# Two half-step FFNs by seven block products: the token sums made feature-major instead of token-major

## The chip, the cores and the metric

The kernel runs on one core of a Trainium2 chip. The metric is the device time of one launch in microseconds, taken as the median of several runs. PE is the matrix engine, DVE the vector engine, ACT the scalar engine, POOL the GpSimd engine, SP the engine whose queue issues most transfers.

## The reference, cut to what matters

One layer of a decoder is computed for 1024 prompt tokens, 16 learned meta tokens and 64 sample tokens (1104 rows of 1024 features, the second half-step 1088 rows):

```
def rms_norm(x, g):
    y = x * rsqrt(mean(x * x, -1) + 1e-6)
    return y * g

def swiglu(x, w_gate, w_up, w_down):          # 1024 -> 2816 -> 1024
    return (silu(x @ w_gate) * (x @ w_up)) @ w_down

def half_ffn(h, g_pre, g_post, w_gate, w_up, w_down):
    return h + 0.5 * rms_norm(swiglu(rms_norm(h, g_pre), w_gate, w_up, w_down), g_post)

h = half_ffn(h, ffn1 ...)                     # first half-step
h = h + rms_norm(token_mixer(...), g)         # DeltaNet and windowed attention, merged by w_out
h = half_ffn(h, ffn2 ...)                     # second half-step
```

## The kernel before

**Seven products.** Each half-step (class `Ffn`) multiplies by blocks in the manner of Strassen and Winograd. The features are cut into halves 1 and 2 (512 each), the tokens into a first half (token tiles 0 to 3 and one half of tile 8) and a second half (tiles 4 to 7 and the other half of tile 8). Tile t of the first half (x) and tile t + 4 of the second half (y) stand at the same columns. Seven operands are made of x1, x2, y1, y2: product 1 takes x1, product 2 x2, product 4 y2, product 5 y1 + y2 - x1 ... by the code, with s = y1 + y2: 5 takes s, 7 takes x1 - y1, 6 takes s - x1, 3 takes x2 - (s - x1). Every operand is feature-major (features on partitions, tokens along the row) and split into a high part and a low part (`x40h`, `x40l`: product 4, columns part 0, high and low), so that three matmuls give an accurate product.

**Making the operands.** The normalised rows of a tile are token-major. `place` (before, L202 to L211) turns 512 features of a tile by four PE transposes into one PSUM buffer (`tr`, four of them in a ring; I call the four transposes a set), ACT copies them to the high part (L210), DVE subtracts to get the low part (L211). `left` does this for x1 and x2 of a first-half tile: two sets. `right` first makes the sums token-major (L230: two on DVE, two on POOL, the POOL ones in place in x) and then turns five things, y2, s, x1 - y1, s - x1 and x2 - (s - x1): five sets, with a yield behind each.

**The order of the work.** PE's order is written by hand: `weave` mixes generators, each with a begin, an end and a count of steps. A half-step begins with `start(0)`, products 1 and 2 of the first column block of gate and up, in two column parts (part 0 needs tiles 0 and 1, part 1 tiles 2, 3 and 8), and `start(1)`, the same of the next column block with both parts in each step. The sets of the tiles are woven in between. In the first half-step that is `tiles_in`: ten steps of `left` before and in part 0 of `start(0)`, then ten steps of `right` (tiles 4 and 5) in part 1, ten (tiles 6 and 7) in `start(1)`, and tile 8's five behind it. Then `up` goes on with products 6, 5, 7, 4, 3, which need all tiles. In the second half-step `right` of tiles 4 and 5 and `left` of 0, 1, 2 and 8 run in `Merge.run`, beside the output projection (matmuls into `dn`) of a later tile, and tiles 6, 3, 8 and 7 in `Merge.rest`, beside `start`. The token tiles of the merge come in the order 0, 4, 1, 5, 2, 8, 6, 3, 7. Tiles 2 and 8 are written to DRAM (`kept`) in `finish` and read again in `rest`, because their place in SBUF is used by others.

**The other engines.** DVE, ACT, POOL and SP each run their queue strictly in the order in which the build's scheduler put it. For each weight block ACT makes the high part (`wh`, L281) and POOL the low part (`wl`, L282). A tile is normalised by a square with row sum on ACT (L81), two small POOL operations (L82, and a power, L83) and a scaling on DVE (L90). In the merge a tile passes through ACT copies out of PSUM, a square, POOL's power, DVE (L623), POOL's addition of the residual (L624), a store to DRAM (L1794), and then L81 to L90 again. DVE also makes the low part of the projection's input (L1750).

Of the kernel before, what the change touches and what calls it, by code (L numbers as in the profile page):

```python
# [13 lines left out]
ALU = mybir.AluOpType  # L14
# [20 lines left out]
def f32(ap):  # L35
    return ap.bitcast(F32)
# [50 lines left out]
def normed(c, pool, x, n, g, dump=None, pin=lambda op: op):  # L87

    r = rstd(c, pool, x, n, 1.0 / D, EPS, "n", dump, pin)
    pin(c.nc.vector.scalar_tensor_tensor(out=x[:n], in0=x[:n], scalar=r[:n, 0:1], in1=g[:n], op0=ALU.mult,  # L90
                                         op1=ALU.mult))
# [79 lines left out]
class Ffn:  # L171
# [28 lines left out]
            lo, hi = self.parts[i]  # L200
            self.X[p][i] = tuple(self.c.t(pool, [P, 4, hi - lo], F32R, tag=f"x{p}{i}{x}") for x in "hl")

    def place(self, psum, p, i, o, src, n):

        c, nc = self.c, self.nc
        ps = c.t(psum, [P, 4, P], tag="tr")
        for k in range(4):
            nc.tensor.transpose(ps[:, k, :n], src[:n, k * P:(k + 1) * P], c.ident[:n, :n])  # L208
        hi, lo = (x[:, :, o:o + n] for x in self.X[p][i])
        nc.scalar.copy(hi, ps[:, :, :n])  # L210
        nc.vector.tensor_tensor(out=lo, in0=ps[:, :, :n], in1=f32(hi), op=ALU.subtract)  # L211

    def where(self, t):

        return (1, 256, self.tail) if t == 8 else (t % 4 // 2, t % 2 * P, P)

    def left(self, psum, x, t):

        i, o, n = self.where(t)
        for p, h in ((1, 0), (2, 512)):  # L220
            self.place(psum, p, i, o, x[:, h:h + 512], n)
            yield

    def right(self, pool, psum, x, y, t):

        nc = self.nc
        i, o, n = self.where(t)
        x1, x2, y1, y2 = x[:n, 0:512], x[:n, 512:], y[:n, 0:512], y[:n, 512:]
        s = self.c.t(pool, [P, 512], tag="sum", bufs=2)[:n]
        op = lambda e, out, a, b, o: e.tensor_tensor(out=out, in0=a, in1=b, op=o)  # L230
        op(nc.vector, s, y1, y2, ALU.add)
        op(nc.vector, y1, x1, y1, ALU.subtract)
        op(nc.gpsimd, x1, s, x1, ALU.subtract)
        op(nc.gpsimd, x2, x2, x1, ALU.subtract)
        for p, src in ((4, y2), (5, s), (7, y1), (6, x1), (3, x2)):
            self.place(psum, p, i, o, src, n)
            yield


    def raw(self, kind, fs, names, pin=lambda op: op):  # L240
# [378 lines left out]
def post_add(c, pool, y, n, g, res, dump):  # L619

    nc = c.nc
    r = rstd(c, pool, y, n, 1.0 / D, 4.0 * EPS, "p", dump)
    nc.vector.scalar_tensor_tensor(out=y[:n], in0=y[:n], scalar=r[:n, 0:1], in1=g[:n], op0=ALU.mult, op1=ALU.mult)  # L623
    nc.gpsimd.tensor_tensor(out=y[:n], in0=y[:n], in1=res[:n], op=ALU.add)  # L624
# [74 lines left out]
class Mixer:  # L699
# [1005 lines left out]


class Merge:
# [80 lines left out]
    def finish(self, t, n, o, dump):  # L1788
        c, nc, pool = self.c, self.nc, self.pool
        t0 = TILES[t][0]  # L1790
        res = c.t(pool, [P, D], tag="res")
        nc.sync.dma_start(res[:n], self.h1_d[t0:t0 + n])
        post_add(c, pool, o, n, self.gain("mix_norm_post", pool), res, dump)
        nc.sync.dma_start(self.h2_d[t0:t0 + n], o[:n])  # L1794
        normed(c, pool, o, n, self.gain("ffn2_norm_pre", pool), res)
        self.o[t] = o
        if t in (2, 8):
            self.kept[t] = c.t(self.f2_d, [P, D], tag="kept", bufs=2)
            nc.sync.dma_start(self.kept[t][:n], o[:n])

    def feed(self, t):

        if t in (4, 5):
            return self.f2.right(self.pool, self.f2.ptr, self.o[t - 4], self.o[t], t), 5
        return self.f2.left(self.f2.ptr, self.o[t], t), 2

    def rest(self):

        pool, right = self.pool, self.f2.right
        x2, x8, y8 = (f32(self.c.t(pool, [P, H, P], F32R, tag=tag)).rearrange("p h t -> p (h t)")  # L1810
                      for tag in ("yl", "yl", "yh"))
        n = self.f2.tail
        for x, src in ((x2, self.kept[2]), (x8[:n], self.kept[8][:n]), (y8[:n], self.kept[8][n:2 * n])):
            self.nc.sync.dma_start(x, src)
        yield from right(pool, self.f2.ptr, x2, self.o[6], 6)
        yield from self.feed(3)[0]
        yield from right(pool, self.f2.ptr, x8, y8, 8)
        yield from right(pool, self.f2.ptr, self.o[3], self.o[7], 7)

# [37 lines left out]
    def run(self, f2, es):  # L1857
        c = self.c
        self.f2, self.o, self.kept = f2, {}, {}
        self.pool = c.pool(es, "mo", bufs=2)  # L1860
        self.f2_d = c.pool(es, "keptd", space=DRAM)
        pso = ExitStack()
        self.psum = c.pool(pso, "pso", space=PSUM, side="right")
        order = (0, 4, 1, 5, 2, 8, 6, 3, 7)
        y = self.load(order[1])
        self.finish(0, P, self.o0, c.t(self.pool, [P, H, P], F32R, tag="yh").rearrange("p h t -> p (h t)"))
        for i in range(1, 9):
            if i == 5:
                f2.ahead(self.pool, "yl")
            now, y = y, self.load(order[i + 1]) if i < 8 else None  # L1870
            done = []
            if i > 1 and order[i - 2] != 6:
                g, n = self.feed(order[i - 2])
                done = [(g, 0.6, 0.95, n)]
            o = c.t(*((self.first, [P, H, P], F32R, "yh") if i % 3 == 0 else (self.pool, [P, H, P], F32R, "o")))
            weave((self.tile_(order[i], *now, f32(o).rearrange("p h t -> p (h t)")), 0, 1, 33 if order[i] == 8 else 49), *done)
        pso.close()


def body(tc, I, O):  # L1880
    nc = tc.nc
    with ExitStack() as es:
        es.enter_context(tc.manual_schedule(engines={mybir.EngineType.PE}))
        c = Ctx(tc)
# [12 lines left out]
        def gain(name, pool):  # L1897
            if name not in gains:
# [289 lines left out]
```

## Time and profile before

| what | value |
|---|---|
| median of 3 runs | 2671.67 us (2671.36, 2671.67, 2674.96) |
| the profiled execution's own time | 2667.11 us |
| its span | 2665.3 us |
| granted PE clock, mean | 0.994 |
| busy: PE, DVE, POOL, ACT | 98%, 58%, 49%, 42% |
| first half-step's start, `start` and the sets of all tiles | 9 to 62 us |
| merge with sets of tiles 0, 4, 1, 5, 2, 8 | 1845 to 1932 us |
| second half-step's `start` with tiles 6, 3, 8, 7 | 1932 to 1970 us |

The profiled execution lies 1.8 us above its span and 4.6 us under the median. A row of a timeline gives the start in us, the busy time in us (of a single instruction, from its start to its end; the next one on the engine can start before), the engine, line, operation and tiles, and in brackets the idle time before it with what ended it. A row of the table by stage gives the stage, the length, and busy time with the count of instructions for PE, PE's weight loads, DVE, ACT, POOL, then the granted clock, the DMA share and GB/s.

### The profile page before, as it was taken

The page shows a single profiled execution, that of the slowest core. Times are in us where ns is not written, and L with a number is a line of the kernel's source. Part 1 is how long each engine was busy: PE and PEld are TensorE (multiplying, and loading weights), DVE is VectorE, ACT ScalarE, POOL GpSimd, SP SyncE. Part 2 cuts the span into 40 slices and gives each one's busy share as a digit, 9 for nine tenths or more (in the row PEclk, how much of TensorE's full clock was granted, in tenths as well). Part 3 has the DMA queues.
Part 4 walks back from the last instruction along what each step waited for, and adds up shares of the span by engine and source line. Part 5 has one row for each costly group of instructions (what it writes and reads, how often), then busy time and mean ns, then how long its engine had stood idle before and what let it go on. Part 6 is the DMA issues. An engine that isn't in the chain of part 4 may idle for free. (4 is left out here: it accounts for less than half of the span.)

```text
span 2665.3 us, 49487 instructions
## 1 busy us (share of the span) xinstructions
PE 2601.2 (98%) x19053; PEld 2478.5 (93%) x19053; DVE 1547.3 (58%) x2299; ACT 1125.8 (42%) x2718; POOL 1293.5 (49%) x1221
## 2 busy tenths in 40 slices
PE   7999999999999999999999999999999999999998
PEld 7999999999988999888889999997799999999998
DVE  7656565545676726995454444444556656654566
ACT  6333343432145634457444444454443434334221
POOL 6656555445526733433343333435555555554471
PEclk9999999999999999999999999999999999999999
DMA  4344343667544754345333333335433434338764
GB/s 164 121 152 153 126 167 117 243 228 252 189 151 149 220 161 132 110 121 171 98 103 89 91 94 100 100 93 160 150 121 139 166 127 149 128 139 317 243 226 144
DMA packets 229568, 406.46 MB, mean 153 GB/s; under 512 B 59750, under 2 KB 121350, under 8 KB 229046
## 3 DMA queue, kind: packets, MB, share of 16 engines
q1 hardware_dynamic: 209030, 324.75, 37.8%
q10 hardware_dynamic: 20304, 78.56, 7.4%
q8 instruction: 150, 2.46, 0.4%
q14 instruction: 84, 0.69, 0.1%
HBM read 264.36 MB, written 140.53 MB: 152 GB/s over the span
## 5 line engine op out<-in xcount | busy, mean ns | idle before, releaser
L132 PE MATMUL gu<-xh,wl 128*128 128x512 f32 (+3 forms) x1456 | 493.6, 339 | 0.0
L128 PE MATMUL gu<-xh,wh 128*128 128x512 f32 (+3 forms) x1456 | 490.5, 337 | 0.0
L130 PE MATMUL gu<-xl,wh 128*128 128x512 f32 (+3 forms) x1456 | 490.3, 337 | 0.0
L282 POOL TENSOR_TENSOR wl<-T,wh 128x512 fp32r<-128x512 f32 x246 | 331.2, 1353 | 320.2 <-ACT wh L281 248.4
L496 PE MATMUL y<-hb,wh 128*128 128x256 f32 (+2 forms) x2528 | 430.5, 290 | 2.4 <-ACT acc L536 1.0
L282 POOL TENSOR_TENSOR wl<-raw,wh 128x512 fp32r<-128x512 f32 x200 | 282.8, 1422 | 249.5 <-ACT wh L281 183.2
L496 PEld LDWEIGHTS y<-hb,wh 128*128 128x128 f32 x2528 | 365.9, 188 | 3.6 <-DVE acc L507 1.4
L281 ACT CAST wh<-T 128x512 fp32r<-128x512 f32 x246 | 152.1, 620 | 364.5 <-PE B L316 111.3
L130 PEld LDWEIGHTS gu<-xl,wh 128*128 128x128 f32 x1456 | 275.9, 190 | 16.7 <-issue 0.6
L128 PEld LDWEIGHTS gu<-xh,wh 128*128 128x128 f32 x1456 | 276.0, 190 | 16.5 <-issue 0.9
L132 PEld LDWEIGHTS gu<-xh,wl 128*128 128x128 f32 x1456 | 276.0, 190 | 16.4 <-issue 0.4
L496 PE MATMUL y<-hb,wl 128*128 128x256 f32 (+2 forms) x1264 | 271.6, 288 | 0.0
L281 ACT CAST wh<-raw 128x512 fp32r<-128x512 f32 x200 | 122.4, 620 | 276.4 <-PE C L316 82.6
L507 DVE TENSOR_TENSOR acc<-acc,y 128x552 f32<-128x552 f32 (+4 forms) x216 | 144.9, 679 | 139.3 <-PE y L496 138.9
L770 POOL TENSOR_TENSOR wl<-raw,wh 128x1024 fp32r<-128x1024 f32 x58 | 139.7, 2409 | 162.0 <-ACT wh L769 132.4
L496 PEld LDWEIGHTS y<-hb,wl 128*128 128x128 f32 x1264 | 207.0, 188 | 0.0
L256 DVE TENSOR_TENSOR T<-raw,raw 128x512 f32<-128x512 f32 x124 | 117.5, 952 | 108.6 <-POOL wl L282 108.6
L1564 POOL TENSOR_TENSOR f<-f,mhalf 128x1 f32<-128x1 f32 (+1 forms) x72 | 54.6, 758 | 125.6 <-DVE f L1562 123.7
L267 DVE TENSOR_TENSOR T<-raw,T 128x512 f32<-128x512 f32 x62 | 65.5, 1060 | 60.8 <-POOL wl L282 60.7
L930 DVE SCALAR_TENSOR_TENSOR cv<-pc,cw,cv 128x1131 f32<-128x1131 f32 x48 | 66.8, 1394 | 31.1 <-POOL cv L927 30.7
L256 DVE TENSOR_TENSOR T<-raw,T 128x512 f32<-128x512 f32 x62 | 63.2, 1027 | 31.9 <-POOL wl L282 31.5
L769 ACT CAST wh<-raw 128x1024 fp32r<-128x1024 f32 x60 | 62.9, 1048 | 32.8 <-PE gu L130 32.8
(593 smaller groups left out, 7325.1 us busy)
## 6 DMA issues: line engine op xcount, KB each, us to landing
hb<-hid SPq DMA_DIRECT2D x71, 552.0 KB
hb<-hid SPq DMA_DIRECT2D x71, 544.0 KB
hid<-hs ACTq DMA_DIRECT2D x69, 552.0 KB
hid<-hs ACTq DMA_DIRECT2D x69, 544.0 KB
raw<-in_w_in_dram SPq DMA_DIRECT2D x58, 512.0 KB
raw<-in_ffn_w_gate_dram SPq DMA_DIRECT2D x100, 256.0 KB
raw<-in_ffn_w_up_dram SPq DMA_DIRECT2D x94, 256.0 KB
raw<-in_ffn_w_down_dram SPq DMA_DIRECT2D x88, 256.0 KB
```

Source lines behind the costliest of these rows:

```text
L128: nc.tensor.matmul(ps, wh, xh, start=first and i == 0, stop=False)
L130: nc.tensor.matmul(ps, wh, xl, start=False, stop=False)
L132: nc.tensor.matmul(ps, wl, xh, start=False, stop=last and i == n - 1)
L256: pin(self.nc.vector.tensor_tensor(out=b[name], in0=b[x], in1=b[y], op=ALU.subtract))
L267: nc.vector.tensor_tensor(out=s, in0=b["21"], in1=s, op=ALU.subtract)
L281: self.nc.scalar.copy(hi, s)
L282: self.nc.gpsimd.tensor_tensor(out=lo, in0=s, in1=f32(hi), op=ALU.subtract)
L496: self.nc.tensor.matmul(self.view(ps[d], (i,)), w[x][:, d * P:(d + 1) * P], hb[:, y, lo:hi], start=j + x + y == 0, stop=j == len(items) - ...
L507: dve = lambda out, x, y: nc.vector.tensor_tensor(out=out, in0=x, in1=y, op=ALU.add)
L769: nc.scalar.copy(hi, raw)
L770: low.tensor_tensor(out=lo, in0=raw, in1=f32(hi), op=ALU.subtract)
L930: nc.vector.scalar_tensor_tensor(out=cv, in0=pc[:, w:w + PADW], scalar=self.cw[:, j, w:w + 1], in1=cv, op0=ALU.mult, op1=ALU.add)
```

## The change

`place` is cut in two: `turned` makes a set, and `place` takes any feature-major source, in PSUM or in SBUF. `left` turns x1 and x2 as before and in addition copies each set, by ACT, over the tile's own token-major values, so that x is kept feature-major in its own place. `right` turns only y2 and y1. The sums are then made feature-major: s3 = x1 - y1 and s2 = y2 - s3 on DVE (one input of each in PSUM, the results in two `sum` buffers, of which there are two in all), x1 + s2 and x2 - s2 on POOL in place in x. Products 7, 6, 5 and 3 are placed from these, from SBUF. A `right` has two steps in place of five, so the weaves of both half-steps take other counts and places. `kept` now holds the feature-major x of tiles 2 and 8 (for tile 8 in pieces of 32 tokens), written behind `left`; tile 8's y rows go to DRAM by themselves.

```
-    def place(self, psum, p, i, o, src, n):
-        ps = c.t(psum, [P, 4, P], tag="tr")
+    def turned(self, psum, src, n):
+        ps = self.c.t(psum, [P, 4, P], tag="tr")
         for k in range(4):
+            self.nc.tensor.transpose(ps[:, k, :n], src[:n, k * P:(k + 1) * P], self.c.ident[:n, :n])
+        return ps[:, :, :n]
+
+    def place(self, p, i, o, src):
+        hi, lo = (x[:, :, o:o + src.shape[2]] for x in self.X[p][i])
+        self.nc.scalar.copy(hi, src)
+        self.nc.vector.tensor_tensor(out=lo, in0=src, in1=f32(hi), op=ALU.subtract)
...
     def left(self, psum, x, t):
-        for p, h in ((1, 0), (2, 512)):
-            self.place(psum, p, i, o, x[:, h:h + 512], n)
+        for p, h, own in zip((1, 2), (0, 512), self.halves(x, n)):
+            ps = self.turned(psum, x[:, h:h + 512], n)
+            self.place(p, i, o, ps)
+            self.nc.scalar.copy(own, ps)
             yield
     def right(self, pool, psum, x, y, t):
-        op(nc.vector, s, y1, y2, ALU.add)
-        op(nc.vector, y1, x1, y1, ALU.subtract)
-        op(nc.gpsimd, x1, s, x1, ALU.subtract)
-        op(nc.gpsimd, x2, x2, x1, ALU.subtract)
-        for p, src in ((4, y2), (5, s), (7, y1), (6, x1), (3, x2)):
-            self.place(psum, p, i, o, src, n)
-            yield
+        y2 = self.turned(psum, y[:, 512:], n)
+        self.place(4, i, o, y2)
+        yield
+        y1 = self.turned(psum, y[:, 0:512], n)
+        op(nc.vector, s3, x1, y1, ALU.subtract)
+        op(nc.vector, s2, y2, s3, ALU.subtract)
+        op(nc.gpsimd, x1, x1, s2, ALU.add)
+        op(nc.gpsimd, x2, x2, s2, ALU.subtract)
+        self.place(7, i, o, s3)
+        self.place(6, i, o, s2)
+        self.place(5, i, o, x1)
+        self.place(3, i, o, x2)
+        yield
...
     def left(self, t):
+        yield from self.f2.left(self.f2.ptr, self.o[t], t)
         if t in (2, 8):
+            x, n = self.o[t], self.f2.where(t)[2]
+            self.kept[t] = self.c.t(self.f2_d, [P, KD, P], tag="kept", bufs=2)
+            self.nc.sync.dma_start(self.kept[t][:, :, :n], x.rearrange("p (k t) -> p k t", t=P)[:, :, :n])
...
-        weave((first, 0, 1, 49), (steps_of(tr, 10), 0.1, 0.9, 10))
-        weave((f1.start(1, False), 0, 1, 49), (steps_of(tr, 10), 0.1, 0.9, 10))
+        weave((first, 0, 1, 49), (steps_of(tr, 4), 0.1, 0.9, 4))
+        weave((f1.start(1, False), 0, 1, 49), (steps_of(tr, 4), 0.05, 0.85, 4))
...
-        weave((steps_of(first, 48), 0, 1, 48), (steps_of(rest, 7), 0.25, 0.95, 7))
-        weave((first, 0, 1, 49), (steps_of(rest, 5), 0.1, 0.8, 5))
-        weave((f2.start(1, False), 0, 1, 49), (steps_of(rest, 5), 0.1, 0.8, 5))
+        weave((steps_of(first, 48), 0, 1, 48), (steps_of(rest, 4), 0.25, 0.9, 4))
+        weave((first, 0, 1, 49), (steps_of(rest, 2), 0.2, 0.7, 2))
+        weave((f2.start(1, False), 0, 1, 49), (steps_of(rest, 2), 0.1, 0.6, 2))
```

The scheduler orders the other engines anew in these stages and nowhere else, but for one transfer of the mixer that changes places with its neighbour. Three places of the new order matter to the prediction.

DVE in the first half-step, where tiles 4 and 5 are placed; `x_416` (before) and `x_415` (after) are the rows of tile 6, whose normalisation is the L90 row. Before:

```order
L211 TENSOR_TENSOR x30l_76<-tr_405,x30h_75 128x4x128
L211 TENSOR_TENSOR x40l_83<-tr_429,x40h_82 128x4x128
L90 SCALAR_TENSOR_TENSOR x_416<-x_416,rn_418,g_ffn_norm_pre_143 128x1024
L211 TENSOR_TENSOR x50l_104<-tr_440,x50h_103 128x4x128
L211 TENSOR_TENSOR x70l_97<-tr_451,x70h_96 128x4x128
```

There the scaling of tile 6 stood directly behind the first low part of tile 5, `x40l`. DVE at the same place after:

```order
L239 TENSOR_TENSOR sum_424<-tr_425,sum_423 128x512
L214 TENSOR_TENSOR x50l_104<-x_36_139,x50h_103 128x4x128
L214 TENSOR_TENSOR x70l_97<-sum_423,x70h_96 128x4x128
L214 TENSOR_TENSOR x30l_76<-x_36_139,x30h_75 128x4x128
L214 TENSOR_TENSOR x60l_111<-sum_424,x60h_110 128x4x128
L214 TENSOR_TENSOR x50l_104<-x_37_141,x50h_103 128x4x128
L90 SCALAR_TENSOR_TENSOR x_415<-x_415,rn_417,g_ffn_norm_pre_143 128x1024
```

It now stands behind `x50l` of tile 5 (the one with `x_37`), which needs POOL's sum of that tile.

POOL at the same place after; `x_36` and `x_37` are tiles 0 and 1, in which the sums of tiles 4 and 5 are made, `rn_417` is tile 6's factor, and "x2" is x1 + s2 with x2 - s2:

```order
L297 TENSOR_TENSOR wl_575<-raw_472,wh_574 128x512
L239 TENSOR_TENSOR x_36_139<-x_36_139,sum_369 128x512 x2
L297 TENSOR_TENSOR wl_623<-raw_476,wh_622 128x512
L82 TENSOR_SCALAR rn_417<-rn_417 128x1
L239 TENSOR_TENSOR x_37_141<-x_37_141,sum_424 128x512 x2
L83 TENSOR_TENSOR rn_417<-rn_417,mhalf_64 128x1
```

Tile 6's power now stands behind both sums of tile 5; before, its two operations followed each other directly.

DVE in the merge after, around the projection input of tile 6 (`yl_22160`, L1765, L1750 before) and the scaling of tile 2 (`o_22057`, L638, L623 before):

```order
L214 TENSOR_TENSOR x20l_21725<-tr_22111,x20h_21724 128x4x128
L638 SCALAR_TENSOR_TENSOR o_22057<-o_22057,rp_22128,g_mix_norm_post_21778 128x1024
L1765 TENSOR_TENSOR yl_22160<-yl_22160,yh_22161 128x1024
L214 TENSOR_TENSOR x40l_21720<-tr_22194,x40h_21719 128x4x128
L239 TENSOR_TENSOR sum_22192<-o_21871,tr_22206 128x512
```

Before, the row of L1750 stood two rows ahead of that of L623; now it stands behind it.

More of the change, by code (lines that the diff above doesn't have):

```diff
@@ L201, in x_tiles, with halves @@
             self.X[p][i] = tuple(self.c.t(pool, [P, 4, hi - lo], F32R, tag=f"x{p}{i}{x}") for x in "hl")
-    def place(self, psum, p, i, o, src, n):
-        c, nc = self.c, self.nc
-        ps = c.t(psum, [P, 4, P], tag="tr")
+    def turned(self, psum, src, n):
+        ps = self.c.t(psum, [P, 4, P], tag="tr")
         for k in range(4):
[L208 to L211, printed above, removed]
+            self.nc.tensor.transpose(ps[:, k, :n], src[:n, k * P:(k + 1) * P], self.c.ident[:n, :n])
[4 more added lines that the diff above has]
+        self.nc.vector.tensor_tensor(out=lo, in0=src, in1=f32(hi), op=ALU.subtract)
     def where(self, t):
         return (1, 256, self.tail) if t == 8 else (t % 4 // 2, t % 2 * P, P)
+    def halves(self, x, n):
+        return [x[:, h:h + 512].rearrange("p (k t) -> p k t", t=P)[:, :, :n] for h in (0, 512)]
     def left(self, psum, x, t):
         i, o, n = self.where(t)
-        for p, h in ((1, 0), (2, 512)):
-            self.place(psum, p, i, o, x[:, h:h + 512], n)
+        for p, h, own in zip((1, 2), (0, 512), self.halves(x, n)):
+            ps = self.turned(psum, x[:, h:h + 512], n)
+            self.place(p, i, o, ps)
+            self.nc.scalar.copy(own, ps)
             yield
@@ L227, in right @@
         i, o, n = self.where(t)
-        x1, x2, y1, y2 = x[:n, 0:512], x[:n, 512:], y[:n, 0:512], y[:n, 512:]
-        s = self.c.t(pool, [P, 512], tag="sum", bufs=2)[:n]
+        x1, x2 = self.halves(x, n)
+        s3, s2 = (self.c.t(pool, [P, 4, P], tag="sum", bufs=2)[:, :, :n] for _ in range(2))
         op = lambda e, out, a, b, o: e.tensor_tensor(out=out, in0=a, in1=b, op=o)
-        op(nc.vector, s, y1, y2, ALU.add)
-        op(nc.vector, y1, x1, y1, ALU.subtract)
-        op(nc.gpsimd, x1, s, x1, ALU.subtract)
-        op(nc.gpsimd, x2, x2, x1, ALU.subtract)
-        for p, src in ((4, y2), (5, s), (7, y1), (6, x1), (3, x2)):
-            self.place(psum, p, i, o, src, n)
-            yield
+        y2 = self.turned(psum, y[:, 512:], n)
[11 more added lines that the diff above has]
+        yield
     def raw(self, kind, fs, names, pin=lambda op: op):
@@ L1796, in finish, with left @@
         self.o[t] = o
-        if t in (2, 8):
-            self.kept[t] = c.t(self.f2_d, [P, D], tag="kept", bufs=2)
-            nc.sync.dma_start(self.kept[t][:n], o[:n])
+        if t == 8:
+            self.kept_y = c.t(self.f2_d, [P, D], tag="kept_y")
+            nc.sync.dma_start(self.kept_y[:n // 2], o[n // 2:n])
     def feed(self, t):
         if t in (4, 5):
-            return self.f2.right(self.pool, self.f2.ptr, self.o[t - 4], self.o[t], t), 5
-        return self.f2.left(self.f2.ptr, self.o[t], t), 2
+            return self.f2.right(self.pool, self.f2.ptr, self.o[t - 4], self.o[t], t)
+        return self.left(t)
+    def left(self, t):
+        yield from self.f2.left(self.f2.ptr, self.o[t], t)
+        if t in (2, 8):
+            x, n = self.o[t], self.f2.where(t)[2]
+            self.kept[t] = self.c.t(self.f2_d, [P, KD, P], tag="kept", bufs=2)
+            self.nc.sync.dma_start(self.kept[t][:, :, :n], x.rearrange("p (k t) -> p k t", t=P)[:, :, :n])
     def rest(self):
@@ L1812, in rest @@
         n = self.f2.tail
-        for x, src in ((x2, self.kept[2]), (x8[:n], self.kept[8][:n]), (y8[:n], self.kept[8][n:2 * n])):
-            self.nc.sync.dma_start(x, src)
+        for x, t, n in ((x2, 2, P), (x8, 8, n)):
+            self.nc.sync.dma_start(x.rearrange("p (k t) -> p k t", t=P)[:, :, :n], self.kept[t][:, :, :n])
+        self.nc.sync.dma_start(y8[:n], self.kept_y[:n])
         yield from right(pool, self.f2.ptr, x2, self.o[6], 6)
-        yield from self.feed(3)[0]
+        yield from self.feed(3)
         yield from right(pool, self.f2.ptr, x8, y8, 8)
@@ L1872, in run @@
             if i > 1 and order[i - 2] != 6:
-                g, n = self.feed(order[i - 2])
-                done = [(g, 0.6, 0.95, n)]
+                done = [(self.feed(order[i - 2]), 0.6, 0.95, 2)]
             o = c.t(*((self.first, [P, H, P], F32R, "yh") if i % 3 == 0 else (self.pool, [P, H, P], F32R, "o")))
```

## Prediction

> **What bounds the kernel now.** I read the page first, then PE's timeline in the stages that the change touches, then the table by stage.
>
> ```profile
> span 2665.3 us, 49487 instructions
> PE 2601.2 (98%) x19053; PEld 2478.5 (93%) x19053; DVE 1547.3 (58%) x2299; ACT 1125.8 (42%) x2718; POOL 1293.5 (49%) x1221
> ```
>
> ```profile
> 1967.14 3.02 PE C L316 x24
> ```
>
> PE is busy 98% of the span; the last line, from the chain that ended last, is the steady state (24 matmuls in 3.02 us, 0.126 each). So an edit pays through PE's own instructions or through PE's waits. PE's waits in the touched stages, and where the first half-step's products 6 begin:
>
> ```profile
> 27.80 0.41 PE L316 MATMUL A<-x11l,wh 128*128 128x296 f32 x1 [1.58 <-DVE x11l L211]
> 61.54 0.39 PE L316 MATMUL B<-x60h,wh 128*128 128x256 f32 x1
> 1894.38 0.63 PE L208 MATMUL tr<-ident,o 128*128 128x128 f32 x4 [0.77 <-DVE x40l L211]
> 1908.94 0.50 PE L132 MATMUL dn<-xh,yl 128*128 128x512 f32 x1 [0.43 <-DVE yl L1750]
> 1940.14 1.09 PE L208 MATMUL tr<-ident,yl 128*128 128x128 f32 x4 [2.07 <-DVE x41l L211]
> 1945.91 0.40 PE L316 MATMUL A<-x11h,wh 128*128 128x288 f32 x1 [1.03 <-ACT x11h L210]
> 1946.63 0.40 PE L316 MATMUL A<-x11l,wh 128*128 128x288 f32 x1 [0.33 <-DVE x11l L211]
> ```
>
> A wait has a second price. The table by stage gives per stretch its length, busy time and count of PE, PEld, DVE, ACT, POOL, then the granted clock, DMA share and GB/s:
>
> ```profile
> 25.30:28.70 3.40, 1.30 (x7) 1.09 (x8) 3.40 (x8) 0.66 (x3) 0.00 (x0) 0.99 0.00 0
> 28.70:32.10 3.40, 3.40 (x17) 3.37 (x16) 2.73 (x3) 1.61 (x3) 3.30 (x3) 0.50 0.00 0
> 57.50:61.50 4.00, 1.91 (x21) 1.54 (x20) 3.18 (x8) 1.13 (x4) 2.53 (x2) 1.00 0.68 249
> 62.80:66.20 3.40, 3.40 (x17) 3.40 (x16) 3.37 (x5) 1.22 (x2) 1.61 (x2) 0.50 0.63 204
> 1936.70:1940.10 3.40, 1.37 (x12) 1.16 (x11) 2.59 (x4) 0.95 (x2) 1.77 (x1) 1.00 0.00 0
> 1940.10:1943.50 3.40, 3.36 (x16) 3.39 (x17) 2.38 (x4) 2.21 (x3) 3.32 (x3) 0.50 0.03 5
> ```
>
> Each stretch in which PE is busy less than half is followed by 3.4 us at a granted clock of 0.50, which loses half of it, 1.7 us.
>
> **The change, part by part.** All times are on the profiled execution's scale, 2667.11; the median is 4.6 higher.
>
> *Sets.* The price of a set of four transposes, from a place where PE has no wait:
>
> ```profile
> 32.15 0.29 PE L316 MATMUL C<-x11h,wl 128*128 128x296 f32 x1
> 32.28 0.60 PE L208 MATMUL tr<-ident,x 128*128 128x128 f32 x4
> 32.64 0.38 PE L316 MATMUL C<-x11h,wh 128*128 128x296 f32 x1
> 32.86 0.29 PE L316 MATMUL C<-x11l,wh 128*128 128x296 f32 x1
> 32.99 0.30 PE L316 MATMUL C<-x11h,wl 128*128 128x296 f32 x1
> ```
>
> From 32.15 to 32.99 PE started three matmuls and a set; matmuls alone start every 0.133 (32.86 to 32.99), so the set costs 0.84 - 3 x 0.133 = 0.44 us. Five right tiles in each of two half-steps lose three sets each: 30 sets, 13.2 us, if PE is the bound wherever they stood. The Trainium skill, "TensorE: Matmul & The Clock Gate", Part 4 (PE-mode transpose), gives about 275 ns for one transpose in a kernel's context; by it the 120 transposes would be an estimated 33 us. The row has four of them in 0.60 busy, so they overlap, and I keep 0.44.
>
> *New work on a shared port.* Before, the low parts (L211) took one input from PSUM. After, those of products 7, 6, 5 and 3 take both from SBUF. What two SBUF inputs on DVE cost beside POOL:
>
> ```profile
> 28.72 1.60 POOL L230 TENSOR_TENSOR x<-sum,x 128x512 f32<-128x512 f32 x1 [3.85 <-DVE x L230]
> 30.40 1.61 POOL L230 TENSOR_TENSOR x<-x 128x512 f32<-128x512 f32 x1
> 29.21 1.65 DVE L230 TENSOR_TENSOR x<-x,x 128x512 f32<-128x512 f32 x1
> 30.79 0.68 DVE L211 TENSOR_TENSOR x40l<-tr,x40h 128x512 fp32r<-128x512 f32 x1
> ```
>
> DVE's sum at 29.21, both inputs in SBUF, ends 0.54 behind the end of POOL's (30.32) and takes 1.65; the low part from PSUM at 30.79 runs beside POOL's next sum in its usual 0.68. So such a DVE instruction and a POOL one exclude each other. The Trainium skill, "SBUF — State Buffer", Who interferes with whom, states this as an exclusive lock for the whole instruction; the rows agree. A right tile had two such DVE instructions and has four now, and their times and POOL's must be added.
>
> *First half-step: +10.5.*
>
> ```profile
> 12.37 0.60 ACT L210 CAST x10h<-tr 128x512 fp32r<-128x512 f32 x1
> 12.84 0.61 ACT L210 CAST x20h<-tr 128x512 fp32r<-128x512 f32 x1
> 13.32 1.09 ACT L81 ACTIVATE dump<-x 128x1024 bf16<-128x1024 f32 x1
> 33.23 1.28 POOL L282 TENSOR_TENSOR wl<-raw,wh 128x512 fp32r<-128x512 f32 x1
> 34.47 1.29 POOL L230 TENSOR_TENSOR x<-x 128x512 f32<-128x512 f32 x1
> 38.18 0.55 POOL L83 TENSOR_TENSOR rn<-rn,mhalf 128x1 f32<-128x1 f32 x1
> 38.94 1.27 DVE L90 SCALAR_TENSOR_TENSOR x<-x,rn,g_ffn_norm_pre 128x1024 f32<-128x1024 f32 x1
> 40.13 0.68 DVE L211 TENSOR_TENSOR x50l<-tr,x50h 128x512 fp32r<-128x512 f32 x1
> ```
>
> (a) Four of `left`'s own copies stand on ACT ahead of tile 2's square. Copies follow each other by 0.48 (12.37, 12.84, 13.32): 1.9 us, so the part 1 that began at 27.80 begins near 29.7. (b) From there PE has 47 matmuls at 0.133, four sets at 0.44, one cold stretch (1.7) and 14 matmuls at 0.127 before tile 6's first set: it asks for tile 6 at 29.7 + 6.3 + 1.8 + 1.7 + 1.8 = 41.3. (c) Tile 6's scaling now stands on DVE behind the `x50l` of tile 5, which needs POOL's sum x1 + s2 of tile 5; that needs s2, which needs one of the two `sum` buffers, free only when tile 4's low parts and POOL's second sum of tile 4 are done. Its power stands on POOL behind both sums of tile 5. ACT's high part of the second weight block stands behind the copy of A (24 matmuls, two sets and the cold stretch behind 29.7), so POOL is done with the low part (1.28) near 36.9, an estimate. From there on the port: POOL four sums at 1.25, one more weight low part at 1.25 and the small operations at 0.75, together 7.0; DVE six low parts at 0.6 and the scaling at 1.25 with waits for the high parts, together 5.4. 36.9 + 12.4 = 49.3, and PE stands for 8.0 us in place of nothing. Without any exclusion only the longer chain counts, and PE would stand 4.2. (d) From 49.3 the remaining port work of tiles 6, 7 and 8 is 6 sums at 1.25, a weight low part at 1.25, and on DVE 10 low parts and two weight sums at 0.6 and one scaling at 1.25, together 17.4 (12 x 0.6 + 1.25 + 7 x 1.25 = 17.2 and a small operation). About 4 us more pass while one waits for the other's result or for PE's set, and the last high and low part of product 6, which DVE has behind everything else, take 1.3. Products 6 begin near 72.0 and not at 61.54: +10.5. PE's 15 removed sets (6.6) vanish in this wait. Bounds: without exclusion, and with tile 6 4.2 late, less the sets, +2.8; with twice the idle, +13. I take 10.5, since the row at 29.21 shows the exclusion.
>
> *Merge: +2 (0 to +3.5).* Six sets (2.6) and the wait of 0.77 at 1894.38 go.
>
> ```profile
> 1907.68 1.21 DVE L1750 TENSOR_TENSOR yl<-yl,yh 128x1024 fp32r<-128x1024 f32 x1
> ```
>
> But PE already waits at 1908.94 for this low part, which ends at 1908.89. PE arriving earlier only waits longer there. The chain to it (tile 2's norm, its residual, the store and load, the squares of tile 8) gets `kept` copies and own copies put ahead, about 1.6 us on ACT and DVE; and tile 2's scaling now stands ahead of tile 6's projection input, 1.27 more of which I count a third. So the wait grows by what the sets gave back and the stage ends 2 later. A wait of 2 could also cost a cold stretch. The Trainium skill, "TensorE: Matmul & The Clock Gate", What's actually happening, has the clock go cold after an idle window of about 3.4 us; by it this wait would be free of that. The row at 1936.70 went cold after a wait of 2.07 with other idle time near it, so I keep 3.5 as the upper end.
>
> *Second half-step's start: -8.6.* In 1932 to 1970 nine sets go (4.0), the wait of 2.07 at 1940.14 goes because `tr` buffers turn over less, and with it the cold stretch (1.7); the waits of 1.03 and 0.33 for tile 3 go if its low part is in time: -9.1. What is late next is that low part:
>
> ```profile
> 1929.44 1.74 POOL L230 TENSOR_TENSOR yl<-sum,yl 128x512 f32<-128x512 f32 x1
> 1934.79 0.55 POOL L83 TENSOR_TENSOR rp<-rp,mhalf 128x1 f32<-128x1 f32 x1
> 1938.12 1.27 DVE L623 SCALAR_TENSOR_TENSOR o<-o,rp,g_mix_norm_post 128x1024 f32<-128x1024 f32 x1
> 1941.84 2.36 POOL L624 TENSOR_TENSOR o<-o,res 128x1024 f32<-128x1024 f32 x1
> ```
>
> Behind tile 7's power (ends 1935.34) DVE does its scaling (1.27), then tile 6's `x41l` and two sums (0.6 each, an input in PSUM), to 1938.5; `x71l` excludes POOL's residual of tile 7 (2.36 from 1936.7) and ends at 1939.7, and tile 3's `x11l` follows at 1940.3. PE, without the waits, asks for it at 1945.91 less 2.07, 1.7, three sets (1.3) and 1.03, at 1939.8. That gives +0.5 back.
>
> Sum: 10.5 + 2 - 8.6 = +3.9, so 2671.0 for the profiled execution and **2675.6** on the median's scale. 0.2%, 5.3 us, is about what a measurement of this kernel can tell from no change.
>
> **The rivals.** *Faster, by PE's own sum.* If the walk in the first half-step is wrong and PE is never late there: 15 sets less the 1.9 of the copies, -4.7; merge -2.6 - 0.77 = -3.4; start -8.6; together -16.7, 2655. For it speaks that DVE, POOL and ACT are 58%, 49% and 42% busy; against it that PE is already 1.58 late at 27.80 with less on those engines. A weaker form, in which the exclusion costs nothing: 2.8 + 0 - 8.6 = -5.8, 2665.9.
>
> *Slower, by the second half-step.* The same exclusion holds tile 3's `x11l`: if POOL's first sum of tile 6 (1.74) too gets the port ahead of `x71l`, `x11l` ends 1.74 + 2.36 = 4.1 later, and the wait brings a cold stretch back (1.7): +5.8 on top of the forecast, 2681.4. It decides as soon as `x11l` of tile 3 ends more than 7.7 us behind the merge's last matmul (near 1932.1); my walk has 8.2. With the first half-step at its ceiling it is 2684.
>
> *The turned sums do nothing to the ends*: gains and losses cancel as in the forecast, but within 5.3 of 2671.67.
>
> **How the numbers follow.** The forecast's sum stands inside the bound of "same" (2666.3 to 2677.0), with its own range 2668 to 2680, from the first half-step's and the merge's bounds. Faster: 0.13 for PE's plain sum, 0.15 for the weaker form, 0.28. The forecast within the bound: 0.38. Slower: 0.34, of which 0.2 is the second half-step's rival and the rest the upper bounds of the first half-step and the merge. The range leaves out the plain sum's 0.13 and some 0.06 above: 2661 to 2685.
>
> **What would show it.** Right: in the changed profile a PE wait of some 8 us near 41 to 50 for tile 6's first set, released by DVE's scaling L90; products 6 near 72; DVE low parts of L214 with two SBUF inputs of 1.2 to 1.9 us beside POOL's sums; 1932 to 1970 shorter by 8 to 9 with no clock of 0.50 in it. Wrong: products 6 at or ahead of 61 (no hold-up), low parts at 0.68 throughout (no exclusion), a `start` in the second half-step that still waits for `x11l`, or a merge that ends earlier by 2 or more.

## The result, and the profile after

The changed kernel takes 2688.70 us (median of 5 runs, 2683.83 to 2693.48) beside 2671.67 for the kernel before: a ratio of 1.0053, with a 95% interval of 1.0042 to 1.0064, slower by some 14 us by the ratio (its interval is 11 to 17) and 17 by the medians. The prediction said 2675.6 and at most 2685. The profiled execution after is 2688.70 itself, its span 2686.9, and it is 21.6 longer than that of before.

The same parts of the page, after:

```profile
span 2686.9 us, 49248 instructions
PE 2594.4 (97%) x18933; PEld 2471.5 (92%) x18933; DVE 1555.3 (58%) x2299; ACT 1135.7 (42%) x2738; POOL 1290.7 (48%) x1221
```

PE has 120 instructions less and is busy 6.8 us less: the sets are gone. Its idle time (the span less the busy time) has grown from 64.1 to 92.5, by 28.4. PE's timeline after, the rows with a wait in the two stages, and the row at which the second one ends:

```profile
30.13 0.61 PE L331 MATMUL A<-x11h,wh 128*128 128x296 f32 x1 [1.87 <-ACT x11h L213]
50.41 1.08 PE L207 MATMUL tr<-ident,x 128*128 128x128 f32 x4 [7.06 <-DVE x L90]
68.65 0.55 PE L331 MATMUL B<-x60h,wh 128*128 128x256 f32 x1 [3.49 <-DVE sum L239]
72.06 0.61 PE L331 MATMUL B<-x61h,wh 128*128 128x296 f32 x1 [2.86 <-ACT x61h L213]
1892.10 0.80 PE L128 MATMUL dn<-xh,yh 128*128 128x512 f32 x1 [5.76 <-ACT yh L1873]
1923.67 0.79 PE L128 MATMUL dn<-xh,yh 128*128 128x512 f32 x1 [8.86 <-ACT o L1870]
1969.80 0.40 PE L331 MATMUL A<-x11h,wh 128*128 128x288 f32 x1 [1.17 <-ACT g L363]
1990.77 0.28 PE L331 MATMUL B<-x60h,wh 128*128 128x256 f32 x1
```

The first four rows are the hold-up of the first half-step that was forecast. Products 6 begin there in two column parts, with `x60h` at 68.65 (61.54 before) and, behind a further wait, with `x61h` at 72.06 (61.76 before). The wait for tile 6 that ends at 50.41 is DVE's and POOL's; DVE, then POOL after:

```profile
39.80 1.77 DVE L214 TENSOR_TENSOR x60l<-sum,x60h 128x512 fp32r<-128x512 f32 x1
48.99 1.27 DVE L90 SCALAR_TENSOR_TENSOR x<-x,rn,g_ffn_norm_pre 128x1024 f32<-128x1024 f32 x1
```

```profile
44.66 3.26 POOL L239 TENSOR_TENSOR x<-x,sum 128x512 f32<-128x512 f32 x2
47.88 1.00 POOL L83 TENSOR_TENSOR rn<-rn,mhalf 128x1 f32<-128x1 f32 x1
```

The power (L83) stands behind both sums of tile 5, and the scaling (L90) begins 0.1 behind its end.

The two waits of some 6 and 9 us in the merge were not: there PE waits to begin the next tile's projection, and is released by ACT's copy of the last tile out of `dn` (two buffers, each for half the features of a tile). In the second half-step's start the waits of 2.07, 1.03 and 0.33 of before have become one of 1.17. The table by stage, first the kernel before, then after; the stages are the merge (first to last projection matmul) and the start (from there to the first matmul of product 6):

```profile
1833.30:1931.90 98.60, 96.74 (x440) 76.49 (x441) 51.00 (x50) 44.75 (x77) 48.24 (x49) 0.98 0.48 156
1931.90:1970.00 38.10, 34.67 (x263) 33.02 (x262) 18.25 (x29) 19.50 (x39) 18.41 (x16) 0.96 0.36 122
```

```profile
1848.80:1960.80 112.00, 97.38 (x416) 76.95 (x417) 51.08 (x47) 48.54 (x85) 44.31 (x48) 0.91 0.43 138
1960.80:1990.80 30.00, 28.78 (x227) 27.80 (x226) 23.85 (x30) 19.30 (x39) 18.95 (x16) 1.00 0.48 151
1886.40:1889.80 3.40, 0.00 (x0) 0.00 (x0) 3.23 (x4) 1.37 (x3) 3.04 (x2) 1.00 0.34 77
1889.80:1893.20 3.40, 1.10 (x3) 0.91 (x4) 1.49 (x2) 2.32 (x4) 0.25 (x1) 0.50 0.00 0
1893.20:1896.60 3.40, 3.40 (x10) 2.63 (x9) 1.89 (x2) 1.14 (x3) 0.97 (x3) 0.50 0.20 28
```

The merge has grown by 13.4, the start has shrunk by 8.1. In the merge PE's clock is 0.91 in the mean: the last two rows show it at 0.50 from 1889.80 to 1896.60. The first 2.3 of these 6.8 us still lie in the first wait; for the other 4.5 the matmuls have begun again and are slow. Around the second wait the clock is at 0.50 from about 1917.1 to 1927.3, of which 3.6 lie behind the wait. The Trainium skill, "TensorE: Matmul & The Clock Gate", What's actually happening, has the clock go cold behind one idle window of about 3.4 us; the trace agrees for this wait (the stretch from 1886.40 has no PE work at all).

With the first matmul of product 5 as the first half-step's mark (66.22 before, 77.65 after), the difference of 21.6 is made of +11.4 in the first half-step, +4.1 up to the merge, +13.4, -8.1, and +0.8 behind it. The 4.1 lie in the mixer, where nothing was changed but two transfers that changed places; the ten experiments below are longer there by 0.7 to 7.1 than the profiled execution before, which lies under all five timed runs of its kernel. So the three stages carry 16.7, about the 17.0 between the medians; that the 4.1 belong to this execution of the kernel before, and not to the change, is argued from this and not shown.

Why PE waits in the merge is read from the engines that come before the copy. PE's last set of tile 4 and of tile 5, then ACT, DVE and POOL after, from tile 4's last set to the copy, with the second copy as ACT's last row (the `yh` of L239, L214 is tile 0's place, where x1 + s2 and x2 - s2 of tile 4 are made; the `yh` that L1873 writes is tile 5, in the same place):

```profile
1884.35 0.60 PE L207 MATMUL tr<-ident,o 128*128 128x128 f32 x4
1913.28 0.60 PE L207 MATMUL tr<-ident,yh 128*128 128x128 f32 x4
```

```profile
1882.69 0.59 ACT L213 CAST x40h<-tr 128x512 fp32r<-128x512 f32 x1 [0.35 <-PE tr L207]
1888.41 0.62 ACT L213 CAST x50h<-yh 128x512 fp32r<-128x512 f32 x1 [1.15 <-POOL yh L239]
1890.08 0.62 ACT L213 CAST x30h<-yh 128x512 fp32r<-128x512 f32 x1 [1.05 <-POOL yh L239]
1891.46 1.07 ACT L1873 COPY yh<-dn 128x512 f32<-128x512 f32 x2 [0.76 <-DVE x30l L214]
1923.03 1.07 ACT L1870 COPY o<-dn 128x512 f32<-128x512 f32 x2 [1.67 <-DVE x30l L214]
```

```profile
1884.00 1.28 DVE L90 SCALAR_TENSOR_TENSOR o<-o,rn,g_ffn_norm_pre 128x1024 f32<-128x1024 f32 x1
1885.92 0.69 DVE L239 TENSOR_TENSOR sum<-tr,sum 128x512 f32<-128x512 f32 x1
1887.30 1.63 DVE L214 TENSOR_TENSOR x60l<-sum,x60h 128x512 fp32r<-128x512 f32 x1
1890.73 0.69 DVE L214 TENSOR_TENSOR x30l<-yh,x30h 128x512 fp32r<-128x512 f32 x1
```

```profile
1886.76 3.30 POOL L239 TENSOR_TENSOR yh<-yh,sum 128x512 f32<-128x512 f32 x2 [3.51 <-DVE sum L239]
```

The copy ends a chain: set, sums on DVE, two sums on POOL, high part, low part of product 3, and only then is the place free. It takes 7.1 us for tile 4 (1884.35 to 1891.46) and 9.75 for tile 5 (1913.28 to 1923.03). The kernel before at the same copy, ACT:

```profile
1871.91 0.59 ACT L1850 COPY yh<-dn 128x512 f32<-128x512 f32 x1 [0.78 <-PE tr L208]
1872.87 0.61 ACT L1850 COPY yh<-dn 128x512 f32<-128x512 f32 x1
```

There the sums were made ahead of the sets, and the last one to read the place was PE's own transposition, so the copy came directly behind it and PE never waited for it; for the copy into tile 1's place it waited 0.26.

### The profile page after: what moved, and what is told of

It is laid out like the page before. It is cut to its first block, busy times and chain, and to the rows that moved or that the text cites. A ratio compares the mean times of both kernels' runs of the same rounds, so it can differ in the third digit from the quotient of the medians.

```text
span 2686.9 us, 49248 instructions
## 1 busy us (share of the span) xinstructions
PE 2594.4 (97%) x18933; PEld 2471.5 (92%) x18933; DVE 1555.3 (58%) x2299; ACT 1135.7 (42%) x2738; POOL 1290.7 (48%) x1221
## 5 line engine op out<-in xcount | busy, mean ns | idle before, releaser
L128 PEld LDWEIGHTS gu<-xh,wh 128*128 128x128 f32 x1456 | 275.7, 189 | 16.7 <-issue 0.9
```

The costliest lines, as they stand in the source:

```text
L128: nc.tensor.matmul(ps, wh, xh, start=first and i == 0, stop=False)
```

## The experiments

Theory A: three separate terms. In the first half-step, the order of the queues and POOL's sums hold up tile 6 and then the products 6; in the merge the places of tiles 0 and 1 are held longer; in the start the sets and waits go. Rival B for the merge: the engines simply have more to do there. Rivals for the first half-step stand with the runs.

**1. The first half-step as before, the second as changed.**

```
-                    yield from f1.right(xin, ptr, xs[-8 if t == 8 else t - 4], xs[t], t)
+                    yield from f1.right_old(xin, ptr, xs[-8 if t == 8 else t - 4], xs[t], t)
...
-        weave((first, 0, 1, 49), (steps_of(tr, 4), 0.1, 0.9, 4))
+        weave((first, 0, 1, 49), (steps_of(tr, 10), 0.1, 0.9, 10))
...
```

> The first half-step is made as before (five sets a right tile, token-major sums, no own copies of left), the second as in the changed kernel. Theory A, that the losses of the two half-steps are separate and add: the products 7, 5 of the first half-step begin at the time of before (66.2 for product 5) and not 11.4 later, while the merge keeps its two waits of some 6 and 9 us; the time is 2688.7 - 11.4 = 2677, between 2674 and 2680. Rival, that what the first half-step loses is partly hidden later (by a transfer or by the mixer's own waits): the gain is under 5, 2684 or more.

Measured: 2680.31 us, ratio to before 1.0025 (1.0015 to 1.0035). Product 5 begins at 67.18, the merge's waits are 5.74 and 7.85, the merge takes 112.1 and the start 29.8. The first half-step is back at its time of before to within 1.0; the time came down by 8.4 where 11.4 was expected, a little over the stated range, and in the profiled execution the merge's first matmul is 7.2 later than before, of which only 1.0 is from this stage and the rest from the mixer. The merge's waits stand without the first half-step's hold-up: the two losses are separate.

**2. The sets of tiles 4 and 5 earlier in the merge.**

```
-                done = [(self.feed(order[i - 2]), 0.6, 0.95, 2)]
+                done = [(self.feed(order[i - 2]), *((0.25, 0.6) if order[i - 2] in (4, 5) else (0.6, 0.95)), 2)]
```

> The changed kernel, with the steps of the right tiles 4 and 5 woven into the merge's tiles at 0.25 to 0.6 and not at 0.6 to 0.95; nothing else moves in the program. Theory A, that PE waits in the merge because tiles 5 and 8 are written to the places of tiles 0 and 1, which are held until the last low part (product 3) of tiles 4 and 5: the places come free some 7 us earlier (0.35 of a tile of 20 us), the wait of 5.76 goes, that of 8.86 falls below 3, the cold stretches behind them go too, and the time is 10 to 14 lower, 2675 to 2679. Rival B, that the merge is longer because ACT, DVE and POOL have more to do there (own copies, low parts that exclude POOL): the work is the same and the time stays within 3 of 2688.7; PE waits elsewhere.

Measured: 2686.45, ratio 1.0055 (1.0042 to 1.0068). The time is in B's range, 2.3 lower by the medians and not lower by the ratio. The rows lie between the two theories: the waits went from 5.76 and 8.86 to 3.99 and 5.51, the merge from 112.0 to 106.3. Counted from the merge's first matmul, tile 4's last set came 4.6 earlier, but the low part that frees the place only 2.5. DVE in this run:

```profile
1882.30 1.66 DVE L214 TENSOR_TENSOR x70l<-sum,x70h 128x512 fp32r<-128x512 f32 x1 [1.43 <-ACT x70h L213]
1883.88 1.77 DVE L214 TENSOR_TENSOR x60l<-sum,x60h 128x512 fp32r<-128x512 f32 x1
1886.17 1.27 DVE L90 SCALAR_TENSOR_TENSOR o<-o,rn,g_ffn_norm_pre 128x1024 f32<-128x1024 f32 x1
1887.37 0.68 DVE L214 TENSOR_TENSOR x30l<-yh,x30h 128x512 fp32r<-128x512 f32 x1
```

The first row waits 1.43 because ACT made that high part behind tile 1's square; two low parts share their time with POOL's sums; and tile 1's scaling came to stand between the low parts. In the rows the direction is A's and the size is not; the time is B's, so B isn't excluded. That needed a run that changes the places and leaves the work.

**3. Tile 6's norm ahead of tile 5's sums in the first half-step.** Its power stands ahead of POOL's sums of tile 5, its scaling ahead of the low parts of that tile (`ahead` is tile 6's norm, called between the sums on DVE and those on POOL).

```
...
+        if ahead:
+            ahead()
+            pin = self.c.tc.keep_in_program_order
+        pin(op(nc.gpsimd, x1, x1, s2, ALU.add))
+        pin(op(nc.gpsimd, x2, x2, s2, ALU.subtract))
+        self.place(7, i, o, s3, pin)
+        self.place(6, i, o, s2, pin)
...
```

> The changed kernel, with tile 6's norm put ahead of the POOL sums and the low parts of tile 5 on ACT, POOL and DVE (issue order pinned). Theory A, that PE's wait at tile 6's first set (7.06 at 50.41) comes from the place of the scaling in DVE's queue and of the power in POOL's: the scaling ends some 3 to 4 earlier, near 46.5, the wait falls to 3 or 4, and products 6 begin 2 to 4 earlier than 72.06; 2685 to 2687. Rival, that the summed time of DVE and POOL on their shared port is the bound: the wait only moves to the products 6, which begin at 71.5 to 72.5, and the time stays at 2688 to 2689.

Measured: 2687.31, ratio 1.0053 (1.0040 to 1.0067). PE's wait is 4.66 at 47.69, the scaling ends at 47.54 in place of 50.26, products 6 (second part) begin at 70.08. So the order is worth 2.7 at the scaling's end, under the 3 to 4 expected; PE's wait is 2.4 shorter, and 2.0 reach the products 6. A time 2 lower can't be told from no change here, the rows can. POOL's sum and the scaling on DVE:

```profile
45.20 3.47 POOL L239 TENSOR_TENSOR x<-x,sum 128x512 f32<-128x512 f32 x2
```

```profile
45.27 2.27 DVE L90 SCALAR_TENSOR_TENSOR x<-x,rn,g_ffn_norm_pre 128x1024 f32<-128x1024 f32 x1 [0.44 <-POOL rn L83]
```

Even with the scaling ahead of the low parts, POOL's sum, which began 0.07 ahead of it, costs it 1.0 (2.27 against 1.27).

**4. The old sums for the first half-step and for tiles 0, 1, 4, 5 of the second.** Only the pairs 2 and 6, 3 and 7, 8 are made feature-major.

```
+            return self.f2.right_old(self.pool, self.f2.ptr, self.o[t - 4], self.o[t], t), 5
...
+        yield from (self.f2.left_old if t < 2 else self.f2.left)(self.f2.ptr, self.o[t], t)
```

> The old sums for the whole first half-step and for tiles 0, 1, 4 and 5 of the second; the feature-major sums only for tiles 2, 3, 8 with 6, 7, 8, in the second half-step's start. Theory A, that the gain of the start (8.1 by the traces) is separate from both losses: the first half-step and the merge's waits are as before, the start from the merge's last matmul to product 6 takes 30 and not 38, and the time is 2671.7 - 8 = 2664, between 2662 and 2666. Rival, that the start gains only because the late merge gives the other engines time ahead of it: the gain is under 3, 2669 to 2672.

Measured: 2664.31, ratio 0.9970 (0.9958 to 0.9981): faster than before, as expected. The merge takes 97.8 and the start 29.8. The start gains as much behind a merge that is not late, so its gain is separate, and it is the change's own.

**5. A fourth place in the merge.** s3 and s2 are put over the turned y, which frees 4 KB a partition for one more place; all engines keep their work. (A tail of 32 columns is the second half-step's, one of 40 the first's.)

```
+        if self.tail == 32:
+            s3, s2 = self.halves(y, n)
...
-            o = c.t(*((self.first, [P, H, P], F32R, "yh") if i % 3 == 0 else (self.pool, [P, H, P], F32R, "o")))
+            o = c.t(*((self.first, [P, H, P], F32R, "yh") if i % 4 == 0 else (self.pool, [P, H, P], F32R, "o", 3)))
```

> The changed kernel, in which the second half-step puts s3 and s2 over the turned y1 and y2 (no sum buffers there), and the room goes to a fourth place for the merge's tiles: tile 5 is written to a place that was never held, and tiles 8, 6, 3, 7 to the places of tiles 4, 1, 5, 2. All work of ACT, DVE, POOL and PE stays. Theory A, that PE's two long waits in the merge come from the places of tiles 0 and 1 being held until the last low part of tiles 4 and 5: both waits go, the merge (first to last projection matmul) is 95 to 100 and not 112, and the time falls by 11 to 15, to 2674 to 2678. Rival B, that the engines' added work (own copies, low parts and sums that exclude each other) is the cause: the waits stay within 3 of 5.8 and 8.9 in sum 14.6, and the time within 3 of 2688.7.

Measured: 2674.11, ratio 1.0003 (0.9994 to 1.0013). The merge takes 96.4. PE's waits in it, behind the first, and ACT's copy into tile 0's place:

```profile
1917.15 0.63 PE L207 MATMUL tr<-ident,yh 128*128 128x128 f32 x4 [1.03 <-DVE yh L90]
1922.88 0.50 PE L132 MATMUL dn<-xh,yl 128*128 128x512 f32 x1 [0.95 <-DVE yl L1768]
1931.47 0.41 PE L207 MATMUL tr<-ident,o 32*128 32x32 f32 x4 [0.86 <-DVE o L90]
```

```profile
1895.40 0.59 ACT L1876 COPY yh<-dn 128x512 f32<-128x512 f32 x1 [2.09 <-DVE x30l L214]
```

Both long waits are gone with the work unchanged, so rival B falls. The chain is no shorter: from tile 4's last set at 1885.82 to the end of its `x30l` at 1895.30 it takes 9.5. The copy behind it is that of tile 2, whose first half is done when PE still has the second to write into the other `dn`. The edit also takes away the two `sum` buffers of this half-step, but these held up nothing: in the changed kernel the sums at 1885.20 and 1913.91 begin directly behind DVE's instruction ahead or the set they need. The place was worth 15.5 of the merge and, by the medians, 14.6 of the time (13 by the ratios).

**6. The first half-step as before, the second changed, with the fourth place.** The edits of runs 1 and 5 together.

> The first half-step as before, the whole second half-step with the feature-major sums and with the fourth place of the run before this. Theory A: no loss in the first half-step, the merge without its six sets and short waits is 2 to 4 shorter than the 98.6 of before, the start 8 shorter: 2658 to 2663, under the 2664.3 of the version that keeps the old sums for tiles 0, 1, 4, 5. Rival B: the merge's waits stay in part, 2668 or more.

Measured: 2658.78, ratio 0.9953 (0.9940 to 0.9965). The merge takes 97.0, the start 29.8. The merge is 1.6 shorter than before and not 2 to 4: six sets less (2.6), but short waits of 2.96 in place of 1.85. It is the fastest of all kernels here.

**7. The own copies of tiles 0 and 1 behind the squares of tiles 2 and 3** (with the edit of run 3).

```
+                    norm(3, c.tc.keep_in_program_order)
+                    for x in f1.owns:
+                        c.tc.keep_in_program_order(nc.scalar.copy(*x))
...
```

> The kernel with tile 6's norm ahead, in which besides the four own copies of tiles 0 and 1 stand behind the squares of tiles 2 and 3 on ACT and not ahead of them. Theory A, that the own copies delay part 1 of the first products by 1.9 (27.80 to 29.7 in the prediction; 30.13 measured): part 1 begins near 28, all behind it moves by as much, products 6 begin near 68 and not near 70, and the time is 1 to 2 under 2687.3. Rival: the copies only move to a place where they hold up tile 2's high parts or the POOL sums; part 1 begins at 29.5 or later and the time stays.

Measured: 2687.21, ratio 1.0057 (1.0045 to 1.0070). Products 6 begin at 69.36 and not 70.08. PE's timeline in this run:

```profile
27.52 0.47 PE L207 MATMUL tr<-ident,x-8_45_157 40*128 40x40 f32 x4 [2.34 <-ACT x L233]
29.52 0.61 PE L338 MATMUL A<-x11l,wh 128*128 128x296 f32 x1 [0.35 <-DVE x11l L214]
```

The rival is right: the low part is used at 29.52, and a set of tile 8 now waits 2.34 for an own copy that frees its `tr` buffer. This copy (L233) is one of tiles 2 and 3, not one of the four that were moved, which are done at 18.7; why it is late was not taken apart. 0.7 of the 1.9 came back at the products 6.

**8. The first half-step's POOL sums on DVE.**

```
-        op(nc.gpsimd, x1, x1, s2, ALU.add)
-        op(nc.gpsimd, x2, x2, s2, ALU.subtract)
+        e = nc.vector if self.tail == 40 else nc.gpsimd
+        op(e, x1, x1, s2, ALU.add)
+        op(e, x2, x2, s2, ALU.subtract)
```

> The changed kernel with all four sums of a right tile on DVE in the first half-step (POOL makes none there). Theory A, that DVE and POOL exclude each other where DVE has two inputs in SBUF and that the sum of both sets PE's wait at tile 6: low parts of 1.7 fall to 0.7, DVE needs two more instructions of 0.6 a tile in place of POOL's 2.5, the scaling of tile 6 ends 2 to 4 earlier than 50.3, products 6 begin 2 to 4 earlier than 72.06, and the time is 2 to 4 lower. Rival, that DVE's own queue is the bound and the exclusion costs little: two tiles ahead of the scaling put 2.4 more into it, which ends at 51 to 53, and the time is 1 to 4 higher.

Measured: 2686.01, ratio 1.0048 (1.0035 to 1.0060). PE, then DVE, around tile 6 and the products 6:

```profile
45.41 0.63 PE L207 MATMUL tr<-ident,x 128*128 128x128 f32 x4 [3.44 <-DVE x L90]
65.59 0.61 PE L332 MATMUL B<-x61h,wh 128*128 128x296 f32 x1 [1.75 <-ACT x61h L213]
```

```profile
39.52 0.68 DVE L214 TENSOR_TENSOR x60l<-sum,x60h 128x512 fp32r<-128x512 f32 x1
44.00 1.27 DVE L90 SCALAR_TENSOR_TENSOR x<-x,rn,g_ffn_norm_pre 128x1024 f32<-128x1024 f32 x1
```

The scaling ends 5.0 earlier than in the changed kernel and products 6 begin 6.5 earlier, more than A said; the low part that shared its time with POOL at 1.77 takes 0.68. The scheduler also moved the scaling ahead here, so against run 3 (2.7 by order) 2.3 is for POOL's sums and the exclusion. The 3.44 that PE still waits are DVE's own queue, which shows no wait from 35.43 to the scaling. Of the 6.5, 6.3 show in the profiled execution and only 2.7 in the median; the interval reaches from 2681 to 2687.

**9 and 10. The first half-step with the new sums for the pairs 2 and 6, 3 and 7, 8 only** (on top of run 6), with the sums on POOL and on DVE.

```
...
+                    yield from (f1.right_old if t < 6 else f1.right)(xin, ptr, xs[-8 if t == 8 else t - 4], xs[t], t)
...
```

> The best version so far (fourth place, first half-step old), but with the feature-major sums also for tiles 2, 3, 8 with 6, 7, 8 of the first half-step; tiles 0, 1, 4, 5 keep the old sums, so that tile 6's scaling stands where it stood before. Theory A, that in the first half-step the loss has two parts, the wait for tile 6 (gone here) and the tail, in which the products 6 wait for the sums of tiles 7 and 8 (POOL's two sums of 3.7 and the low parts behind them): PE asks for tile 6 without a long wait, nine sets (4.0) are saved, but from tile 6's first set to the products 6 it takes the 20 to 21 of the changed kernel; they begin at 62 to 64 and the time is 0 to 3 above 2658.8. Rival, that the tail's waits were only the first wait's echo: products 6 begin at 58 to 60 and the time is 2 to 4 lower than 2658.8.

> The same, with the two POOL sums of tiles 6, 7 and 8 of the first half-step on DVE; DVE's order is the same up to tile 6's low part of product 7. Theory A, that POOL's sums and their exclusion of DVE make the tail: the products 6 begin 1.5 to 4 earlier than with the sums on POOL, at 59 to 61.5, and the time is 1 to 3 under it. Rival, that the tail is only the chain behind the last set (sum, high part, low part): they begin within 1 of the run with POOL.

Measured: 2665.24, ratio 0.9982 (0.9971 to 0.9992), and 2663.09, ratio 0.9966 (0.9952 to 0.9979). PE in both, first with POOL, then with DVE:

```profile
59.16 0.36 PE L360 MATMUL B<-x60h,wh 128*128 128x256 f32 x1 [3.41 <-DVE sum L268]
62.57 0.61 PE L360 MATMUL B<-x61h,wh 128*128 128x296 f32 x1 [3.05 <-ACT x61h L213]
```

```profile
59.46 0.55 PE L361 MATMUL B<-x60h,wh 128*128 128x256 f32 x1 [3.71 <-DVE sum L268]
61.77 0.62 PE L361 MATMUL B<-x61h,wh 128*128 128x296 f32 x1 [1.75 <-ACT x61h L213]
```

No wait is left for tile 6, and the tail's two waits are there all the same (3.41 and 3.05; 3.49 and 2.86 in the changed kernel): they are not an echo. The second part of products 6 begins at 62.57 (the first, at 59.16, stops for it), inside A's 62 to 64; the time is not inside A's 0 to 3 above run 6. Nine sets are saved and spent again in the tail, so this half-step gains nothing. POOL's part of the tail is 0.8 (62.57 less 61.77), not the 1.5 to 4 expected, which is the second run's rival; most of the tail is the chain of set, sums, high and low part behind the last set. The two runs came out 6.5 and 4.3 above run 6, of which the stage explains 0.7 to 1.5 (product 5 at 67.54 and 66.77 against 66.05); the rest lies in the unchanged mixer and stays open.

## Why the prediction was wrong

**Sets.** Right: 120 fewer PE instructions, and where PE had no long new wait the time came back. In run 6 the merge has six sets less (2.6 at 0.44) and 1.1 more of short waits: 1.5 less by this sum, 1.6 measured.

**First half-step, +10.5: right in size and path, not in its parts.** Measured +11.4. The walk said part 1 at 29.7, tile 6 asked for at 41.3, its scaling done at 49.3, products 6 at 72.0; the rows have 30.13, 43.35 (50.41 less 7.06), 50.26 and 72.06. The last is the second part of products 6, which was at 61.76 before; the first begins at 68.65. That the total fits better than its parts is luck: tile 6 is asked for 2.0 later than the walk said and waits 0.9 less. Runs 3, 8 and 9 bear out the path: at the scaling's end the order of the queues is worth 2.7 and POOL's sums with the exclusion 2.3, DVE's own queue leaves 3.44 of wait in run 8, and then comes a tail of its own. The Trainium skill, "SBUF — State Buffer", Who interferes with whom, which the prediction leaned on, is borne out by the pairs 1.77 and 0.68 for one low part and 2.27 and 1.27 for one scaling. The exclusion, put at 3.8 (8.0 less 4.2), was put too high: the 2.3 hold it and POOL's sums together.

**Merge, +2 (0 to +3.5): wrong, and this is 11.4 of the 12.8 that the sum is off.** The step that failed is "PE already waits at 1908.94 for this low part": it took the wait that was last before for the one that would be last after. That wait is gone after. The prediction followed `kept` and the two `sum` buffers, and never asked who frees the place into which the next tile is copied: it put that term at nothing without a reason. The change takes the last reading of tile 0's and tile 1's places from PE's transposition to the end of a chain over four engines (7.1 us for tile 4, 9.75 for tile 5). PE's idle time in the merge has grown by 12.8 (two waits of 14.6, less short ones of 1.86 before), and its busy time by 0.6, since the slow clock takes more than the six sets gave back: +13.4. Run 5 shows the cause: one more place takes both waits away while the chain stays.

**Second half-step's start, -8.6: right, but for its last term.** Measured -8.1, and 8.1 to 8.3 shorter in every kernel with the new sums there. Nine sets (4.0), 2.3 less of waits and the slow stretch (1.7) come to 8.0; no clock of 0.50 is in the stage. The wait for `x11l` that was put at +0.5 is another one: PE asks at 1968.63, `x11l` is done at 1968.88, and PE stands until 1969.80 for ACT's `g`, 1.17 in all.

**Sum.** With 13.4 for the merge's 2, the same sum gives 10.5 + 13.4 - 8.6 = 15.3 and 2687 on the median's scale. The slower rival had the side right and the place wrong: tile 3's `x11l` ended 7.9 behind the merge's last matmul, past the 7.7 that the rival named, and it cost nothing, since `g` came later. The range was also less well worked than the sum. The bounds of the first half-step don't follow from its terms (twice the idle of 4 would give +14.5 and not +13; 36.9 + 7.0 is 2.6 behind 41.3 and not 4.2), and with both lower bounds the range would begin at 2665.9 and not 2668. The time lies outside either way. Of the signs that the prediction named for being right, all came true; none of them looked at the merge.

## What to carry to other kernels

When a change moves the last reader of a buffer from one engine to the end of a chain over several, ask who writes that buffer next and who waits for that writer, even where no step of the change names it; a ring of places that was just long enough is part of the critical path. A wait that is last before is not the one that will be last after, so each release in a touched stage needs its own new time. And a change that gains in one stage and loses in two is best taken apart by stage: here the same sums are worth 8 us in the second half-step's start, and the version that keeps them in the second half-step alone, with one more place, is 0.47% faster than before.

## What the runs showed of the hardware beyond this

The price of a wait is not always one slow stretch. With the wait of 5.76 came 6.8 us at a granted clock of 0.50, of which 4.5 lie behind the wait's end, and with that of 8.86 some 10.2, of which 3.6 do; the wait of 1.17 in the start left the clock at 1.00. Of the pairs of stretches in the prediction the second is not adjacent: from 61.50 to 62.80, between its two rows, PE is busy throughout at 1.00. And the profiled executions differ by up to 7.1 us in the unchanged mixer between kernels; no run here settles what from.
